# Moving the sigmoid of the state space gates from the gate products to the merge of the branches

## The chip, the cores and the metric

The kernel runs on one core of a Trainium2 chip. The metric is the device time of one execution in microseconds (us). Five engines work side by side, each taking its own instructions in order: TensorE (PE in the rows; PEld is its weight load), VectorE (DVE), ScalarE (ACT), GpSimd (POOL) and SyncE (SP). POOL, SP and ACT also issue DMAs; a "q" behind an engine's name (ACTq, POOLq) marks what its sequencer does without being busy.

## The reference, cut to what matters

A decoder layer for 256 tokens of width 2048 in float32. A state space branch and an attention branch read the same normed input; each is multiplied per channel by a sigmoid gate, and the sum goes through `w_out`.

```python
h = rmsnorm(x, attn_norm_w[l])
proj = h @ w_in[l]
z, xbc, dt_raw, q, k, v, g = jnp.split(proj, pts, axis=-1)
y_ssm = ssd_mixer(z, xbc, dt_raw, ...) @ w_ssm_out[l]
...
y_attn = moba_attention(q, k, v, ...) @ w_attn_out[l]
g_ssm, g_attn = jnp.split(jax.nn.sigmoid(g + b_gate[l]), 2, axis=-1)
x = x + (g_ssm * y_ssm + g_attn * y_attn) @ w_out[l]
...
x = x + (jax.nn.silu(u_gate) * u_up) @ w_down[l]
```

## The kernel before

**Weights.** All activations lie transposed, channels on partitions and 256 tokens along the row. Products are made in three passes so as to keep float32 precision: a weight is split in a rounded high part (`whi`, made by ACT at L180) and the remainder (`wlo`, made by DVE at L181), and TensorE does high by high (L212), high by low (L213) and low by high (L215). `unit` (L170) loads 1 MB of weights on SP's queue into one of three buffers `wraw` and splits it in two chunks of 1024 columns; `whi` and `wlo` have three buffers each, so ACT and DVE can work up to three chunks ahead of PE. One chunk is 24 matmuls.

**The stages.** First the attention branch, its gates (L561, `gate_attn`) and its output, which is stored pair by pair in DRAM (`ma`). Then the state space branch in nine steps (L837). Steps 0 to 7 make the projections of one of eight groups of heads (`group_units`) while the core work of the group before (`core_steps`: silu, transposes, decay by exponentials at L753, the output products at L769 and L770, a norm with a logarithm and an exponential at L299 and L300) is laid between the units by `sp.tick()`. The gates of this branch are 16 products: `gate_ssm` (L828), four in step 1, four in step 2 and eight in step 8, beside the core work of groups 0, 1 and 7. A gate ends with one activation on ACT (L831), from PSUM into half of a buffer `g`; each pair of gates (128 x 2 x 256) is stored to DRAM by POOL (L833, `gs`). ACT needs another table for a sigmoid than for an exponential or a silu; the line of an `ACT_TABLE_LOAD` is that of the activation it is for.

**The merge.** The last quarter of the product with `w_ssm_out` is eight units (L872), each with `merge` (L860) behind it. For pair u, POOL loads the stored gates `g` (L864) and the stored attention output `a` (L865); DVE adds the unit's sums to `yacc` (L866), multiplies by the gates (L867) and adds the attention part (L868); ACT rounds the result into `mt` (L869) and DVE makes its remainder (L870). `g` and `a` share three buffers, as `gpair` did before. So the gates of pair u+1 are loaded into the buffer that L870 of pair u-1 has just left, and `a` of pair u+1 into the one that L867 of pair u has left. Then follow the 16 units of `w_out` (L885), which read all 16 blocks of `mt`; of the first two units the first halves (blocks 0 to 7) are done before the second halves.

**The order.** The program gives the tiles and their dependencies; a planner sets the order on each engine ahead of time, by when it expects operands to be ready, earlier lines first among what is ready. An engine then takes its instructions in that order and waits where an operand is not there. The table loads are put in afterwards, before each activation whose table is not the loaded one.

Of the kernel before, what the change touches and what calls it, by code (L numbers as in the profile page):

```python
# [10 lines left out]
AF = mybir.ActivationFunctionType  # L11
# [147 lines left out]
def _body(tc, nc, d, out):  # L159
    V, S, PE = nc.vector, nc.scalar, nc.tensor  # L160
# [56 lines left out]
    def cm_unit(src, xh, xl, nk=16):  # L217
        parts = unit(src, nk * 128)
        ps = mm_tile()[:, :T]
        for c in range(2):  # L220
            cm_chunk(ps, parts[c], xh, xl, c * nk // 2, nk // 2, c == 0, c == 1)
        return ps
# [30 lines left out]
    def sm(name, i=0, n=1, rows=slice(0, 128)):  # L253
        o, _ = _SMALL[name]
        return small[rows, o + i:o + i + n]
# [297 lines left out]
    def gate_half(o):  # L553
        if o % 2 == 0:
            gpair[o // 2] = gate_pool.tile([128, 2, T], F32, name="g", bufs=3)
        return gpair[o // 2][:, o % 2]
# [38 lines left out]
    for o in range(KT):  # L595
# [4 lines left out]
        g = gl.pop(o)  # L600
# [16 lines left out]
    o = (KT + 10) * T  # L617
# [210 lines left out]
    def gate_ssm(o):  # L828
        pg = cm_unit(d["wgs"][o], hnh, hnl)
        g = gate_half(o)  # L830
        S.activation(g, pg, AF.Sigmoid, bias=sm("b_gate", o))  # L831
        if o % 2:
            nc.gpsimd.dma_start(gs[o // 2], gpair.pop(o // 2))  # L833

# [2 lines left out]
    for step in range(9):  # L837
        if step < 8:
            for i in group_units(step):
                sp.tick()  # L840
        outs = [(((step - 3) // 2), ((step - 3) % 2) * 4 + u) for u in range(4)] if step >= 3 else []
        ng = {1: 4, 2: 4, 8: 8}.get(step, 0)
        for _ in range(ng):
            gate_ssm(go)
            go += 1
            sp.tick()
        for q, u in outs:
            out_unit(q, u, acc_done(q))
            sp.tick()
        sp.flush()  # L850
        if step < 8:
            nu = 14
            if step == 7:
                nu = 10
            sp.add(core_steps(step), nu)
# [4 lines left out]
    def merge(u, ps):  # L860
        os_ = slice(2 * u, 2 * u + 2)
        g = gate_pool.tile([128, 2, T], F32, name="g", bufs=3)
        a = gate_pool.tile([128, 2, T], F32, name="g", bufs=3)
        nc.gpsimd.dma_start(g, gs[u])  # L864
        nc.gpsimd.dma_start(a, ma[u])  # L865
        V.tensor_tensor(yacc[:, os_], ps, yacc[:, os_], op=ADD)  # L866
        V.tensor_tensor(yacc[:, os_], yacc[:, os_], g, op=MUL)  # L867
        V.tensor_tensor(a, yacc[:, os_], a, op=ADD)  # L868
        S.activation(mh_[:, os_], a, AF.Copy)  # L869
        V.tensor_tensor(ml_[:, os_], a, mh_[:, os_].bitcast(F32), op=SUB)  # L870

    for u in range(8):  # L872
        out_unit(3, u, merge)
# [116 lines left out]
```

## Time and profile before

| | before |
|---|---|
| median of 3 runs | 2036.89 us (2035.17 to 2037.4) |
| the profiled execution | 2035.77 us, span of its instructions 2033.9 us |
| PE busy | 2026.2 us of the span |
| DVE, ACT, POOL busy | 1475.6, 1196.9, 43.4 us |
| DMA | 407.56 MB, 200 GB/s over the span |

A row of the timeline has the start, the duration, the engine, the line, the operation with its tiles and shapes, and in brackets how long the engine had been idle before it and what ended that. Matmuls are pipelined, so the distance between starts tells more of PE's pace than the duration of one. A stretch of PE is best measured from the start of one L215 group to that of the next, which is one chunk.

### The profile page before, as it was taken

The numbers are of one execution on the slowest core, as the hardware profiler recorded it, in microseconds if no ns is written. First come the engines' busy times: TensorE is split into PE (matmuls) and PEld (weight loads), VectorE is DVE, ScalarE is ACT, GpSimd is POOL, SyncE is SP. The second block draws the span as 40 slices with busy tenths as digits, with TensorE's granted clock in tenths as the row PEclk, the third lists the DMA queues.
The fourth block names the chain that finished last, engine by engine and source line by source line (L and its number), as shares of the span: only waits on it lengthen the run. The fifth ranks groups of instructions, "written<-read, shape, count | busy, mean of one in ns | idle before, by whom it ended". The sixth has DMA issues, their size and how long they took to land.

```text
span 2033.9 us, 39479 instructions
## 1 busy us (share of the span) xinstructions
PE 2026.2 (100%) x16539; PEld 1969.0 (97%) x16539; DVE 1475.6 (73%) x2225; ACT 1196.9 (59%) x1686; POOL 43.4 (2%) x83
## 2 busy tenths in 40 slices
PE   9999999999999999999999999999999999999999
PEld 7888889999999999999999999999999999999999
DVE  7567777556688898888989887677777765677554
ACT  6456556444668768667666755565555553455333
POOL 0000000000000000000000010000000000000000
PEclk9999999999999999999999999999999999999999
DMA  7654445655555556555565575555555555555554
GB/s 283 253 192 157 174 173 197 224 209 197 201 202 199 200 205 207 189 192 195 192 206 192 207 286 214 189 190 201 191 191 201 189 193 202 187 194 200 187 185 169
DMA packets 65690, 407.56 MB, mean 200 GB/s; under 512 B 7799, under 2 KB 10408, under 8 KB 21992
## 3 DMA queue, kind: packets, MB, share of 16 engines
q1 hardware_dynamic: 55384, 376.56, 51.5%
q0 software_dynamic: 6528, 22.12, 3.4%
q10 hardware_dynamic: 3600, 6.37, 0.9%
q8 instruction: 129, 2.11, 0.4%
q14 instruction: 49, 0.40, 0.1%
HBM read 398.63 MB, written 9.53 MB: 201 GB/s over the span
## 4 chain that ended last, share of the span: by engine, by line
PE 97%; ACT 1%; DVE 1%; DMA 0%; issue 0%; SPq 0%; DVEq 0%
PE mm L215 27%; PE mm L212 27%; PE mm L213 27%; PE mm L371 4%; PE mm L365 4%; PE mm L366 4%; PE cc L769 1%; PE cc L226 0%; PE cc L227 0%; PE cc L225 0%; DVE wlo L181 0%; PE cc L464 0%; PE cc L770 0%; PE cc L722 0%; ACT whi L180 0%; DMA wraw<-wv 0%
## 5 line engine op out<-in xcount | busy, mean ns | idle before, releaser
L180 ACT ACTIVATE whi<-wraw 128x1024 fp32r<-128x1024 f32 (+1 forms) x712 | 745.6, 1050 | 705.9 <-PE mm L213 556.8
L181 DVE TENSOR_TENSOR wlo<-wraw,whi 128x1024 fp32r<-128x1024 f32 (+1 forms) x712 | 858.7, 1209 | 275.7 <-ACT whi L180 270.7
L212 PE MATMUL mm<-hn,whi 128*128 128x256 f32 x1536 | 359.3, 277 | 1.7 <-ACT whi L180 1.7
L213 PE MATMUL mm<-hn,whi 128*128 128x256 f32 x1536 | 358.7, 276 | 0.0
L213 PE MATMUL mm<-fh,whi 128*128 128x256 f32 x1408 | 327.8, 276 | 0.0
L212 PE MATMUL mm<-fh,whi 128*128 128x256 f32 x1408 | 327.8, 276 | 0.0
L212 PEld LDWEIGHTS mm<-hn,whi 128*128 128x128 f32 x1536 | 288.4, 188 | 3.7 <-ACT whi L180 2.5
L213 PEld LDWEIGHTS mm<-hn,whi 128*128 128x128 f32 x1536 | 288.4, 188 | 0.1
L213 PEld LDWEIGHTS mm<-fh,whi 128*128 128x128 f32 x1408 | 264.3, 188 | 0.0
L212 PEld LDWEIGHTS mm<-fh,whi 128*128 128x128 f32 x1408 | 264.3, 188 | 0.0
L215 PE MATMUL mm<-hn,wlo 128*128 128x256 f32 x1536 | 205.9, 276 | 0.4 <-DVE wlo L181 0.4
L215 PEld LDWEIGHTS mm<-hn,wlo 128*128 128x128 f32 x1536 | 188.6, 188 | 0.8 <-DVE wlo L181 0.8
L215 PE MATMUL mm<-fh,wlo 128*128 128x256 f32 x1408 | 188.2, 276 | 0.0
L215 PEld LDWEIGHTS mm<-fh,wlo 128*128 128x128 f32 x1408 | 172.7, 188 | 0.0
L213 PE MATMUL mm<-a,whi 128*128 128x256 f32 x704 | 164.3, 276 | 0.0
L212 PE MATMUL mm<-a,whi 128*128 128x256 f32 x704 | 164.3, 276 | 0.0
L365 PE MATMUL mm<-whi,hp 128*128 128x512 f32 x384 | 152.1, 396 | 0.8 <-ACT whi L195 0.8
L366 PE MATMUL mm<-whi,hp 128*128 128x512 f32 x384 | 150.5, 392 | 0.0
L212 PEld LDWEIGHTS mm<-a,whi 128*128 128x128 f32 x704 | 132.1, 188 | 0.0
L213 PEld LDWEIGHTS mm<-a,whi 128*128 128x128 f32 x704 | 132.1, 188 | 0.0
L212 PE MATMUL mm<-yt,whi 128*128 128x256 f32 x512 | 119.4, 276 | 0.0
L213 PE MATMUL mm<-yt,whi 128*128 128x256 f32 x512 | 119.3, 276 | 0.0
(299 smaller groups left out, 3186.9 us busy)
## 6 DMA issues: line engine op xcount, KB each, us to landing
wraw<-wup SPq DMA_DIRECT2D x88, 1024.0 KB, 4.8
wraw<-wssd SPq DMA_DIRECT2D x80, 1024.0 KB, 4.8
wraw<-wqk SPq DMA_DIRECT2D x32, 1024.0 KB, 4.8
wraw<-wso SPq DMA_DIRECT2D x32, 1024.0 KB, 4.8
wraw<-wd SPq DMA_DIRECT2D x32, 1024.0 KB, 4.8
wraw<-wga SPq DMA_DIRECT2D x16, 1024.0 KB, 4.8
wraw<-wao SPq DMA_DIRECT2D x16, 1024.0 KB, 5.0
wraw<-wgs SPq DMA_DIRECT2D x16, 1024.0 KB, 4.8
```

The lines of the kernel that those rows point to most:

```text
L180: last_hi[0] = S.activation(hi[:, :n // 2], raw[:, s], AF.Copy)
L181: V.tensor_tensor(lo[:, :n // 2], raw[:, s], hi[:, :n // 2].bitcast(F32), op=SUB)
L212: PE.matmul(ps, w, xh[:, k0 + k], start=first and k == 0, stop=False)
L213: PE.matmul(ps, w, xl[:, k0 + k], start=False, stop=False)
L215: PE.matmul(ps, lo[:, k * 128:(k + 1) * 128], xh[:, k0 + k], start=False, stop=last and k == nk - 1)
L365: PE.matmul(pst[tt], hph[:, k0 + k, ts], wh, start=first and k == 0, stop=False)
L366: PE.matmul(pst[tt], hpl[:, k0 + k, ts], wh, start=False, stop=False)
L371: PE.matmul(pst[tt], hph[:, k0 + k, ts], wl, start=False, stop=last and k == 1)
L769: PE.matmul(ps, x0, m[:, :, h, 0:256], start=True, stop=False)
```

## The change

The gate's activation becomes an Identity with the same bias, so that what is stored in DRAM is the biased product. In `merge`, ACT applies the sigmoid in place to each pair of gates when it has been loaded, ahead of the three DVE operations of that pair.

```diff
@@ def gate_ssm(o):
         pg = cm_unit(d["wgs"][o], hnh, hnl)
         g = gate_half(o)
-        S.activation(g, pg, AF.Sigmoid, bias=sm("b_gate", o))
+        S.activation(g, pg, AF.Identity, bias=sm("b_gate", o))
         if o % 2:
             nc.gpsimd.dma_start(gs[o // 2], gpair.pop(o // 2))
@@ def merge(u, ps):
         nc.gpsimd.dma_start(g, gs[u])
         nc.gpsimd.dma_start(a, ma[u])
+        S.activation(g, g, AF.Sigmoid)
         V.tensor_tensor(yacc[:, os_], ps, yacc[:, os_], op=ADD)
         V.tensor_tensor(yacc[:, os_], yacc[:, os_], g, op=MUL)
         V.tensor_tensor(a, yacc[:, os_], a, op=ADD)
```

## Rows read from the trace of the kernel before

**Rows 1.** The page, part 1: busy us of each engine, share, instructions

```profile
PE 2026.2 (100%) x16539; PEld 1969.0 (97%) x16539; DVE 1475.6 (73%) x2225; ACT 1196.9 (59%) x1686; POOL 43.4 (2%) x83
```

**Rows 2.** Waits of PE: who waited for whom: us in total, times, longest

```profile
PE mm L212 <- ACT whi L180: 1.7, 2, 1.1
```

**Rows 3.** Timeline of PE, chunks in an undisturbed stretch of step 7

```profile
1052.12 1.07 PE L215 MATMUL mm<-hn,wlo 128*128 128x256 f32 x8
1054.84 1.07 PE L215 MATMUL mm<-hn,wlo 128*128 128x256 f32 x8
...
1058.29 1.07 PE L215 MATMUL mm<-hn,wlo 128*128 128x256 f32 x8
```

**Rows 4.** Timeline of PE in step 8: first and last chunk, the waits

```profile
1124.90 1.07 PE L215 MATMUL mm<-hn,wlo 128*128 128x256 f32 x8
...
1127.23 0.39 PE L212 MATMUL mm<-hn,whi 128*128 128x256 f32 x1 [0.56 <-ACT whi L180]
...
1132.13 0.38 PE L212 MATMUL mm<-hn,whi 128*128 128x256 f32 x1 [1.10 <-ACT whi L180]
...
1137.62 1.21 PE L215 MATMUL mm<-hn,wlo 128*128 128x256 f32 x8 [0.43 <-DVE wlo L181]
...
1155.81 1.07 PE L215 MATMUL mm<-hn,wlo 128*128 128x256 f32 x8
```

**Rows 5.** Timeline of PE in step 2, beside the gates there

```profile
690.66 1.07 PE L215 MATMUL mm<-hn,wlo 128*128 128x256 f32 x8
...
693.75 1.10 PE L215 MATMUL mm<-hn,wlo 128*128 128x256 f32 x8
```

**Rows 6.** Timeline of ACT in step 8, first and last of five table loads

```profile
1114.44 1.28 ACT L831 ACT_TABLE_LOAD   x1
...
1129.36 1.28 ACT L831 ACT_TABLE_LOAD   x1
...
1131.03 1.05 ACT L180 ACTIVATE whi<-wraw 128x1024 fp32r<-128x1024 f32 x1
```

**Rows 7.** Timeline of DVE in step 8

```profile
1127.21 1.23 DVE L181 TENSOR_TENSOR wlo<-wraw,whi 128x1024 fp32r<-128x1024 f32 x1 [1.37 <-ACT whi L180]
```

**Rows 8.** Groups of ACT by line: count, busy us, mean ns, idle before

```profile
L753 ACT ACTIVATE m<-m 128x768 f32<-128x768 f32 x32 | 26.9, 841 | 0.4
...
L682 ACT ACTIVATE slotA<-mm,small 128x256 f32<-128x256 f32 x24 | 13.2, 549 | 0.0
...
L831 ACT ACT_TABLE_LOAD x10 | 12.8, 1283 | 0.2
...
L753 ACT ACT_TABLE_LOAD x5 | 6.4, 1283 | 0.1
```

**Rows 9.** Timeline of one unit of the merge, DVE, POOL and ACT

```profile
1202.16 0.68 DVE L870 TENSOR_TENSOR mt<-g,mt 128x512 fp32r<-128x512 f32 x1
...
1203.13 0.54 POOL L864 DMA_DIRECT2D g<-gs  x1 [1.93 <-DVE mt L870]
...
1205.26 1.06 ACT L180 ACTIVATE whi<-wraw 128x1024 fp32r<-128x1024 f32 x1 [1.67 <-PE mm L213]
...
1206.58 0.63 ACT L869 ACTIVATE mt<-g 128x512 fp32r<-128x512 f32 x1 [0.25 <-DVE g L868]
...
1207.97 1.06 ACT L180 ACTIVATE whi<-wraw 128x1024 fp32r<-128x1024 f32 x1 [0.76 <-PE mm L213]
...
1210.57 0.69 DVE L867 TENSOR_TENSOR slotA<-slotA,g 128x512 f32<-128x512 f32 x1
1210.70 1.06 ACT L180 ACTIVATE whi<-wraw 128x1024 fp32r<-128x1024 f32 x1 [1.67 <-PE mm L213]
```

**Rows 10.** Loads of the gates at L864: us from issue to landing

```profile
DMA to landing us min/median/max: 5.6/5.8/6.8
```

**Rows 11.** Last L870 of the merge; a chunk of `w_out` on PE

```profile
1229.36 0.68 DVE L870 TENSOR_TENSOR mt<-g,mt 128x512 fp32r<-128x512 f32 x1
1229.48 1.07 PE L215 MATMUL mm<-mt,wlo 128*128 128x256 f32 x8
```

## The prediction, before the result was known

> **What bounds the kernel now.** I read the page's busy rows first: PE is busy for 2026.2 of 2033.9 us [rows 1], so the time is what TensorE has to compute plus the few places where it is kept waiting. No edit here touches a matmul. The whole question is which waits of PE go and which come. Second, the waits of PE: the largest is for the rounded weight halves that ACT makes at L180, 1.7 us in two places [rows 2]. Third, PE's timeline around those places. The yardstick is the distance from the first low-half matmul (L215) of one chunk of weights to that of the next: 2.72 us for a plain chunk, 3.45 us where the four matmuls of one pair of state-space heads stand between, so 0.73 us for these [rows 3]. In the last stage of the state space branch, 1124.90 to 1155.81, PE does nine chunks and the matmuls of four pairs: 9 x 2.72 + 4 x 0.73 = 27.40 us of work in 30.91 us [rows 4]. So 3.51 us are lost there. The three waits shown make 0.56 + 1.10 + 0.43 = 2.09 us of it; the other 1.42 us are restarts and matmuls that stand farther apart than elsewhere, whose cause no row shows. A second, smaller place is at 690.66: a chunk of 3.09 us, 0.37 us too long [rows 5].
>
> Fourth, ACT in that stretch. The two late halves follow on table loads: a gate (L831) loads the sigmoid's table, the next exponential of the decay (L753) loads its own again, 1.28 us each, five loads in turn from 1114.44 to 1129.36, and the rounding at 1131.03 stands behind them [rows 6]. PE takes it up at 1132.13 [rows 4]. Besides 690.66 this is the only place where a table load of the gates reaches PE.
>
> **Part 1: the gates lose their sigmoid.** The instruction stays, on the same tile with the same bias, so its own time hardly changes. Its table load goes: ten of 1.28 us, and with them the five that L753 needs to get the exponential back, 19.2 us of ACT in all [rows 8]. An Identity with a bias stands in the same stages at L682 [rows 8], and no table load has that line, so the new form costs no load. Of the 19.2 us only what held PE counts: the 3.51 us and, at most, the 0.37 us. Before the wait at 1132.13 ACT has by then spent five loads since 1114.44, 6.4 us; the waits of PE up to there come to 1.66 us, so ACT would be early. The wait for a low half at 1137.62 is DVE catching up after those late halves, so it should go too. Bounds for the gain: below, the 2.09 us of plain waits; above, 3.51 + 0.37 = 3.88 us. I take **3.5 us**, nearer to the upper end, since matmuls keep their distance where ACT is early [rows 3]; both ends stay in the range. What is late next there is DVE, which has the decay and the output products to do; but there it waits for ACT, not the other way about: 1.37 us ahead of the low half at 1127.21 [rows 7].
>
> **Part 2: eight sigmoids in the merge.** Each works on 128x512 in SBUF. The trace has no such sigmoid: the copy of the same width at L869, 0.63 us [rows 9], and an exponential of 768 columns, 0.84 us [rows 8], bound it; I take 0.65 us, by the copy. Eight make 5.2 us, and one table load 1.28 us. ACT has room: in a unit of 5.44 us (two chunks) it does two roundings of 1.06 us and one copy of 0.63 us [rows 9], 2.75 us, and would then do 3.4. By its length alone this part costs nothing; if the cover were gone it would cost 6.5 us.
>
> **Part 3: the wait that the sigmoid brings.** ACT takes its instructions in order, and now one of them waits for a load from DRAM. The load of the gates of pair u+1 is issued on POOL only when the buffer is free, 0.29 us after L870 of pair u-1 ends, at 1203.13 for example [rows 9]; it lands 5.6 to 6.8 us later, 5.8 in the median [rows 10], here at 1208.93. Its user L867 starts at 1210.57 [rows 9]. So there are 1.64 us between landing and use, and the sigmoid takes 0.65 of them: enough, if ACT turns to it then. Behind the waiting sigmoid stand the roundings of the next chunks, for which PE waits, and the copy L869, for which DVE waits, which for its part frees the buffer of the next load. What it costs hangs on its place in ACT's order, which the trace of before can't show. The four places within one unit are these, from rows 9:
>
> - after the rounding at 1207.97, before that at 1210.70: the data has landed, ACT is idle, nothing is late: 0 us.
> - between the copy at 1206.58 and the rounding at 1207.97: the sigmoid and then that rounding wait till 1208.93, some 1.4 to 1.6 us. A rounding has 0.9 + 2 x 2.72 - 1.06 = 5.3 us to spare, as it is made three chunks ahead. But DVE has its low half in front of L867, so the chain of loads gets 1.4 us later every second unit, 4.1 us by the last. The last L870 ends at 1230.04, and the second half of the first w_out unit, which starts 0.91 us after 1229.48, reads it as the last two of its eight blocks, twelve matmuls in, at 1231.75 [rows 11]: 1.7 us to spare. Cost 4.1 - 1.7 = 2.4 us.
> - ahead of the copy at 1206.58: a loop closes: L870, load 0.29 + 5.8, sigmoid 0.65, copy 0.63, L870 with gaps 0.8: 8.2 us a unit in place of 5.44. Six loads depend on it: 6 x 2.8 = 16.8 us late, less 1.7: **15 us**.
> - ahead of the rounding at 1205.26 as well: another 1.06 us a unit, 6 x 3.86 - 1.7 = 21.5 us.
>
> The loads of the second operand (L865) wait for L867 as before and move with it; POOL gets no instruction more. The first two pairs are loaded long before the stage; their sigmoids may stand in front of the last group's norm, for one table load and two sigmoids at most, 2.6 us of a chain that I can't price, taken as 0 with 2.6 left in the range.
>
> I take 0 us for part 3: the sigmoid's place is set where its operand is expected, and every earlier place needs the load to be expected within some 3.7 us of L870 (1202.84 to 1206.58), where the chip takes 6.1. But this is the weakest step.
>
> The Trainium skill (DMA: Bandwidth & Descriptors, Anatomy of one DMA) gives 2.0 us plus bytes over 436e3 for a load issued by GpSimd, an estimate of 2.6 us for these 256 KB. By that the operand would be there before the copy, the loop of the third place would be shorter than a unit and cost 0. The trace differs, with 5.8 us [rows 10], and the measurement decides.
>
> **The sum.** The profiled execution took 2035.77 us, 1.9 us around its span; the median of the three is 2036.89. From the median: 2036.89 - 3.5 + 0 = **2033.4 us**. About 0.2% (4.1 us, so below 2032.8 or above 2041.0) is what a measurement of this kernel can tell from no change; the whole gain lies at that bound.
>
> **Rivals.**
> - The sigmoid one place earlier, after the copy: 2036.89 - 3.5 + 2.4 = 2035.8. For it: the copy is the last work of a pair and ACT is idle behind it till 1207.97 [rows 9]. Chance 0.22.
> - Slower: the sigmoid ahead of the copy L869, so that the loop through the load sets the pace from the third pair on: 2036.89 - 3.5 + 15 = 2048.4, up to 2051. For it: the load is slow, 5.8 us [rows 10], so an order made with any shorter time in mind puts the sigmoid too early, and ACT is idle ahead of 1205.26 and of 1206.58 [rows 9]. Against it: only a time under 3.7 us does it. It decides from a place ahead of 1206.58. Chance 0.22; with the rounding behind it too, 2054.9, chance 0.10.
> - The gates do lose their table, but DVE holds PE in the same stretch, or as much is lost in front of the norm: 2036.9. Against it: DVE's own wait for ACT [rows 7]. Chance 0.10.
>
> **How the numbers follow.** The forecast has the remaining 0.36, its own range 2032.3 to 2035. Faster by over 0.2% needs the full upper bound of part 1: something under half of that, 0.17. Slower by over 0.2% is the two places ahead of the copy: 0.32. The rest, 0.51, is within. The range from 2032.2 to 2051 leaves out the 0.10 of the worst place and some 0.07 at its foot and in between.
>
> **What would show it.** Part 1: no table load at L831 or, between the gates, at L753; no wait of PE on L180 between 1112 and 1156, nine chunks and four pairs there in 27.4 us. Part 2: one sigmoid load in the merge. Part 3: ACT idle ahead of the new line, released by the load of g; its start against the copy L869; the distance between two L870, 5.44 or 8.2 us; PE's first w_out chunks waiting for the merge's tile. The forecast is wrong if PE waits in the merge at all.

## The result, and the profile after

The changed kernel takes **2051.19 us** in the median of six executions (2044.77 to 2056.58); the kernel before, beside it, takes 2035.65 us (2034.9 to 2037.4). The ratio is 1.0072 with the interval 1.005 to 1.0094: slower by 0.7%, some 15 us. Here and below a ratio leaves out executions in which the whole program ran markedly longer and a median does not, so the two can differ a little. The time lies 0.2 us above the upper end of the forecast's range, and of the four places listed in part 3 the trace shows the third and, for two pairs, the fourth.

The profiled execution took 2044.98 us with a span of 2043.2 us, one of the two shortest of the six. What is said below of its stretches explains 9.3 us over the span before (2033.9), not the median's 15. In the changed kernel the lines of the merge are one higher: the new sigmoid is L866, the operations on DVE L867 to L869, the copy into `mt` L870, its remainder L871.

The page, part 1 (busy us of each engine, share of the span, instructions):

```profile
PE 2029.5 (99%) x16539; PEld 1972.8 (97%) x16539; DVE 1475.9 (72%) x2225; ACT 1178.3 (58%) x1677; POOL 43.5 (2%) x83
```

Beside [rows 1], ACT has lost 18.6 us and nine instructions: eight sigmoids have come and, counted by line, 17 table loads have gone (the fifteen of [rows 8] and four at the norms, L299 and L300, less two new ones at L866). The span grew though ACT works less, so the waits come next. The waits (who waited for whom, us in total, times, longest):

```profile
PE mm L212 <- ACT whi L180: 8.0, 3, 4.0
...
ACT g L866 <- DMA g<-gs: 19.3, 6, 5.1
ACT L866 <- DMA g<-gs: 6.6, 1, 6.6
```

The second and third rows have no like before: the new line makes ACT stand still for 26 us, waiting for the load of the gates. The first is the row of [rows 2], 1.7 us then. ACT by line (count, busy us, mean ns, idle before and what ended it):

```profile
L866 ACT ACTIVATE g<-g 128x512 f32<-128x512 f32 x8 | 5.1, 632 | 19.3 <-DMA g<-gs 19.3
L866 ACT ACT_TABLE_LOAD x2 | 2.6, 1283 | 6.6 <-DMA g<-gs 6.6
```

No table load stands at L831 any more, where [rows 8] have ten, nor at L753. A sigmoid takes 632 ns.

**Where the time was won.** PE's timeline from step 8 to the first chunks of `w_out`; the first two rows are the ends of the stretch of [rows 4]:

```profile
1124.19 1.07 PE L215 MATMUL mm<-hn,wlo 128*128 128x256 f32 x8
...
1151.61 1.07 PE L215 MATMUL mm<-hn,wlo 128*128 128x256 f32 x8
...
1196.76 1.07 PE L215 MATMUL mm<-yt,wlo 128*128 128x256 f32 x8
1201.78 0.38 PE L212 MATMUL mm<-yt,whi 128*128 128x256 f32 x1 [3.95 <-ACT whi L180]
...
1204.78 1.61 PE L215 MATMUL mm<-yt,wlo 128*128 128x256 f32 x8
...
1208.12 1.10 PE L215 MATMUL mm<-yt,wlo 128*128 128x256 f32 x8
...
1230.73 1.10 PE L215 MATMUL mm<-mt,wlo 128*128 128x256 f32 x8
1235.22 0.39 PE L212 MATMUL mm<-mt,whi 128*128 128x256 f32 x1 [3.39 <-ACT whi L180]
...
1237.69 1.91 PE L215 MATMUL mm<-mt,wlo 128*128 128x256 f32 x8
...
1241.55 1.07 PE L215 MATMUL mm<-mt,wlo 128*128 128x256 f32 x8
```

The first two rows bound the same nine chunks and four pairs as in [rows 4]: 27.42 us, where 30.91 stood and 27.40 was reckoned. At 1151.61 PE is 1155.81 - 1151.61 = 4.20 us ahead of the kernel before: 3.49 us from this stretch and 0.71 that it already had at 1124.19.

**Where it was lost again.** The rest of that timeline, in stretches from one L215 to another, against 2.72 us a chunk (its first stretch is not among the rows shown):

| stretch of PE | takes | work | lost |
|---|---|---|---|
| 1170.89 to 1183.16, in front of the last group's norm | 12.27 | 4 x 2.72 | 1.39 |
| 1196.76 to 1204.78 | 8.02 | 2.72 | 5.30 |
| 1204.78 to 1208.12 | 3.34 | 2.72 | 0.62 |
| 1208.12 to 1230.73 | 22.61 | 8 x 2.72 | 0.85 |
| 1230.73 to 1237.69 | 6.96 | 2.72 | 4.24 |
| 1237.69 to 1241.55 | 3.86 | 2.72 | 1.14 |

The sum is 13.5 us; less the lead of 4.2 it is 9.3, the difference of the spans. Of the 13.5 us, 7.3 are the two long waits themselves (3.95 + 3.39); the other 6.2 are restarts, matmuls at a slower pace, and the first line.

**What held PE.** ACT's timeline in the merge:

```profile
1198.34 1.28 ACT L866 ACT_TABLE_LOAD   x1 [6.58 <-DMA g<-gs]
1199.63 0.63 ACT L866 ACTIVATE g<-g 128x512 f32<-128x512 f32 x1
1200.17 0.61 ACT L870 ACTIVATE mt<-g 128x512 fp32r<-128x512 f32 x1
1200.69 2.94 ACT L180 ACTIVATE whi<-wraw 128x1024 fp32r<-128x1024 f32 x3
...
1224.14 0.63 ACT L866 ACTIVATE g<-g 128x512 f32<-128x512 f32 x1 [4.02 <-DMA g<-gs]
1224.67 1.04 ACT L180 ACTIVATE whi<-wraw 128x1024 fp32r<-128x1024 f32 x1
1225.62 0.62 ACT L870 ACTIVATE mt<-g 128x512 fp32r<-128x512 f32 x1
...
1233.08 0.63 ACT L866 ACTIVATE g<-g 128x512 f32<-128x512 f32 x1 [4.94 <-DMA g<-gs]
```

Read the lines in order: a sigmoid of pair u+1 that waits for its load, and behind it the copy L870 of pair u. Of the six pairs that this concerns (2 to 7) five stand so; only pair 4's sigmoid comes behind the copy. For pairs 2, 5 and 7 the copy follows at once, as at 1200.17: the third place of part 3. For pairs 3 and 6 a rounding stands between, as at 1224.67: the fourth. At 1200.69 three roundings follow at one go: they had queued up behind the wait, and PE takes the first of them at 1201.78, 3.95 us late. The loop closes on DVE and POOL:

```profile
1219.20 0.69 DVE L871 TENSOR_TENSOR mt<-g,mt 128x512 fp32r<-128x512 f32 x1 [1.05 <-ACT mt L870]
1220.19 0.54 POOL L864 DMA_DIRECT2D g<-gs  x1 [2.83 <-DVE mt L871]
...
1226.89 0.69 DVE L871 TENSOR_TENSOR mt<-g,mt 128x512 fp32r<-128x512 f32 x1
```

L871 frees the buffer at 1219.89, POOL issues the load at 1220.19, the sigmoid starts at 1224.14, the copy at 1225.62, the next L871 at 1226.89: 7.69 us for one turn (with the rounding of 1224.67 in it), and 7.37 for the next, in place of 5.44 for a unit. All seven distances are 9.62, 6.95, 4.08, 7.36, 7.69, 7.37 and 4.80 us, 47.9 in all for 38.1. The last L871 starts at 1239.06, before it was 1229.36 [rows 11].

### The profile page after: what moved, and what is told of

Its sections match the earlier page's. It is cut to its first block, busy times and chain, and to the rows that moved or that the text cites. A ratio compares the mean times of both kernels' runs of the same rounds, so it can differ in the third digit from the quotient of the medians.

```text
span 2043.2 us, 39477 instructions
## 1 busy us (share of the span) xinstructions
PE 2029.5 (99%) x16539; PEld 1972.8 (97%) x16539; DVE 1475.9 (72%) x2225; ACT 1178.3 (58%) x1677; POOL 43.5 (2%) x83
## 4 chain that ended last, share of the span: by engine, by line
PE 95%; DMA 2%; issue 2%; DVE 1%; ACT 1%; POOL 0%; SPq 0%; DVEq 0%; ACTq 0%; POOLq 0%
PE mm L212 26%; PE mm L213 26%; PE mm L215 26%; PE mm L371 4%; PE mm L365 4%; PE mm L366 4%; DMA g<-gs 1%; PE cc L769 1%; PE cc L226 0%; PE cc L227 0%; PE cc L225 0%; DMA wraw<-wso 0%; PE cc L464 0%; PE cc L770 0%; PE cc L722 0%
## 5 line engine op out<-in xcount | busy, mean ns | idle before, releaser
L215 PE MATMUL mm<-hn,wlo 128*128 128x256 f32 x1536 | 205.5, 276 | 0.0
L215 PEld LDWEIGHTS mm<-hn,wlo 128*128 128x128 f32 x1536 | 188.4, 188 | 0.0
L215 PE MATMUL mm<-fh,wlo 128*128 128x256 f32 x1408 | 188.2, 276 | 0.0
L215 PEld LDWEIGHTS mm<-fh,wlo 128*128 128x128 f32 x1408 | 172.7, 188 | 0.0
```

The source lines that it names most:

```text
L215: PE.matmul(ps, lo[:, k * 128:(k + 1) * 128], xh[:, k0 + k], start=False, stop=last and k == nk - 1)
```

## The experiments

The theory to be tested: **the wait**. The gates' part of the change wins some 4 us, the sigmoid's length costs nothing, and the loss is ACT standing behind the load, by the place of the sigmoid in ACT's order. The rivals: **length and table**, that eight sigmoids and a table load more in the merge are what PE feels; and **lead paid back**, that what the gates give is lost again behind them, whatever the merge does. Every diff is against the changed kernel. Ratios are to the kernel before in the same rounds, whose median was 2036.24 us beside the experiments 1, 2, 3 and 4 and 2036.53 beside the others.

**1. The gates alone.** No sigmoid in the merge, so the sigmoid of these gates is left out of the computation altogether.

```diff
@@ def merge(u, ps):
-        S.activation(g, g, AF.Sigmoid)
```

> The gates' half of the change alone: the gates are stored without the sigmoid and the merge has no sigmoid either, so the sigmoid of the state space gates is left out of the computation. In the trace of the changed kernel PE reaches the first chunk of the last quarter at 1157.05, against 1161.24 before: 4.2 us early. Wait theory (the whole loss is ACT waiting in the merge for loads, because the sigmoid stands ahead of the copy of the pair before): 2035.7 - 4.2 = 2031.5 us, and no wait of PE from 1100 to 1240. Rival (the earlier lead comes only from work that has moved and is paid back later in the branch): 2035 to 2036 us. Either way no table load at L831 or L753.

Measured: 2032.42 us, ratio 0.9982 (0.997 to 0.9995), by the ratio 3.7 us faster. The waits of PE hold nothing of the stretch any more; these are all that are listed:

```profile
PE cc L267 <- DVE onesr L260: 1.1, 1, 1.1
PE mm L365 <- ACT whi L195: 0.7, 1, 0.7
PE cc L508 <- DVE sums L499: 0.2, 1, 0.2
```

The lead is kept to the end, so the third theory falls: 0.9982 lies off 1, and nothing is paid back behind the gates. The whole loss of the change, 1.0072 - 0.9982 = 0.0090 or 18.3 us by the ratios, hangs on the one line in the merge. The nine chunks and four pairs take 27.41 us here too (1126.00 to 1153.41), though PE enters them 1.10 us later than in the kernel before and leaves them 2.40 us earlier. So the 3.5 us of this stretch repeat, and the rest of the 4.20 us of lead in the changed kernel does not.

**2. The sigmoid behind a rounding.** All instructions, loads and buffers stay; the unit of pair u+2 is built within `merge` of pair u, and the sigmoid of pair u is put behind the first rounding of that unit. That is the first place of part 3, where the forecast had expected it. (The lines that keep hold of that rounding are left out of the diff.) One thing more moves with it, the unit's own place in the program; experiment 3 pins the sigmoid without that.

```diff
@@ def merge(u, ps):
-        S.activation(g, g, AF.Sigmoid)
+        ahead[u + 2] = unit(d["wso"][3, u + 2] if u < 6 else d["wout"][u - 6])
+        with tc.issue_after(first_hi[0].ins):
+            S.activation(g, g, AF.Sigmoid)
...
-        out_unit(3, u, merge)
+        out_unit(3, u, merge, ahead[u])
```

> The changed kernel with one order more: the sigmoid of pair u stands behind the first rounding of the unit two further on, so it is the place that the prediction priced at 0. Same instructions, same loads, same buffers. Wait theory: ACT reaches the sigmoid when the load has landed, its waits for g fall from 26 us to under 3, two L871 (the remainders of mt) stand 5.44 us apart again, 2031.5 us, up to 2033. Rival (the length of the eight sigmoids and their table load in a stage where DVE is 88% busy is what costs, or the load itself is too slow): as the changed kernel, 2045 to 2057 us.

Measured: 2032.2 us, ratio 0.9984 (0.997 to 0.9999). It is below both kernels, and with the sigmoid kept it is as fast as without one. What ACT waits for the gates, in all:

```profile
ACT g L871 <- DMA g<-gs: 2.0, 3, 0.8
```

And a unit on ACT's timeline (rounding L182, sigmoid L871, copy L875 in this kernel):

```profile
1197.00 0.63 ACT L875 ACTIVATE mt<-g 128x512 fp32r<-128x512 f32 x1 [0.25 <-DVE g L874]
1198.40 1.07 ACT L182 ACTIVATE whi<-wraw 128x1024 fp32r<-128x1024 f32 x1 [0.77 <-PE mm L216]
1200.29 0.63 ACT L871 ACTIVATE g<-g 128x512 f32<-128x512 f32 x1 [0.83 <-DMA g<-gs]
```

Copy, rounding, sigmoid: the load has had the copy and a rounding's time to land, and from the second on the remainders of the pairs stand 5.44 us apart again (5.63 for the last). The sigmoids of the first two pairs come behind the last group's norm here, at 1184.41 and 1188.49, so nothing is lost in front of it either. The same eight sigmoids and the same loads cost 19 us in one order and nothing in another. Length cannot be the cause.

**3. The sigmoid behind the copy.** The second place of part 3.

```diff
@@ def merge(u, ps):
-        S.activation(g, g, AF.Sigmoid)
+        with tc.issue_after(lastm[0].ins) if lastm[0] is not None else contextlib.nullcontext():
+            S.activation(g, g, AF.Sigmoid)
...
-        S.activation(mh_[:, os_], a, AF.Copy)
+        lastm[0] = S.activation(mh_[:, os_], a, AF.Copy)
```

> The changed kernel with the sigmoid of pair u put behind the copy into mt of pair u-1: one place later than in the changed kernel, and the second place of the prediction's list. Wait theory with that list: the gain of 4.2 us less 2.4 us, 2033.9 us (2032 to 2037), ACT waiting some 1.5 us for each load but not longer from pair to pair. Rival (length or load): 2045 to 2057 us. If the time is at 2045 or more, the loop through the copy is not what costs.

Measured: 2038.18 us, lowest 2035.41, ratio 1.0001 (0.9983 to 1.0018). That is 0.0019 over experiment 1, 3.9 us, with intervals that overlap. The median lies 1.2 us above the expected range; the ratio makes it 2036.4 us, within. Between the two profiled executions with a pinned order, this one and experiment 2, the difference is 2035.41 - 2031.88 = 3.5 us. Its waits and PE's timeline:

```profile
PE mm L212 <- ACT whi L180: 2.8, 1, 2.8
...
ACT g L869 <- DMA g<-gs: 8.4, 5, 2.4
```

```profile
1223.31 1.07 PE L215 MATMUL mm<-mt,wlo 128*128 128x256 f32 x8
1227.14 0.38 PE L212 MATMUL mm<-mt,whi 128*128 128x256 f32 x1 [2.77 <-ACT whi L180]
...
1229.08 1.07 PE L215 MATMUL mm<-mt,wlo 128*128 128x256 f32 x8
```

One chunk takes 5.77 us where 2.72 are due, at the end of the merge, as the list had it: ACT's 8.4 us of waits shift the chain a little with each unit till `w_out` is reached. The three orders give 0, 3.5 to 3.9 and some 18 us, for 2.0, 8.4 and 26 us of ACT's waits: the loss grows with the wait.

**4. Buffers of their own for the gates.** The load no longer waits for L871 of the pair before last; the order is left to the planner.

```diff
@@ def merge(u, ps):
-        g = gate_pool.tile([128, 2, T], F32, name="g", bufs=3)
+        g = sd.tile([128, 2, T], F32, name="ab", bufs=2)
```

> The changed kernel with the gates loaded into two buffers of their own (those of the decay rows, free by then), so that the load of pair u+2 is issued after L868 of pair u and no longer after L871; the attention part keeps the other three. The order is left to the planner. Wait theory: the load comes a whole unit earlier than it is used and the copy into mt no longer leads back to the load, so PE waits at most 1 us in the merge: 2031.5 to 2033 us. Rival (length): 2045 to 2057 us.

Measured: 2035.48 us, ratio 1.0008 (0.9981 to 1.0036): the loss of the change is gone, but the gain of the gates is not there, and the expectation missed by 2.5 us. ACT's waits for the gates are down to 2.9 us and none of PE's is listed in the merge. The order on ACT, however, came out otherwise, at the end of the merge and within it:

```profile
1214.92 1.07 ACT L180 ACTIVATE whi<-wraw 128x1024 fp32r<-128x1024 f32 x1 [0.76 <-PE mm L213]
1216.20 0.63 ACT L866 ACTIVATE ab<-ab 128x512 f32<-128x512 f32 x1 [0.21 <-DMA ab<-gs]
...
1229.83 0.51 ACT L897 ACTIVATE fh<-x,small 128x256 fp32r<-128x256 f32 x1 [4.80 <-DVE x L896]
```

```profile
1233.71 1.21 PE L215 MATMUL mm<-mt,wlo 128*128 128x256 f32 x8
1236.64 1.11 PE L215 MATMUL mm<-mt,wlo 128*128 128x256 f32 x8
...
1315.79 1.11 PE L215 MATMUL mm<-fh,wlo 128*128 128x256 f32 x8
1316.73 0.39 PE L284 MATMUL cc<-ssp,onesr 128*128 128x512 f32 x1
```

The planner itself has put the sigmoids of pairs 2 to 7 behind a rounding, the first place of part 3 (one is shown), and those of the first two pairs long before the norm, at 1129.91 and 1131.40. And the first operation of `w_out`'s epilogue (L897) now stands ahead of two roundings, so that ACT is idle for 4.80 us. PE comes through with one short interruption at 1233.71, and from there on runs 28 chunks in 79.15 us, 2.83 each, instead of 76.16: 3.0 us, though nothing waits. So the earlier start of the load took the loss away together with the order that made it; this kernel can't tell the two apart, and its new order has a price of its own.

**5. The sigmoid in both places.** The gates keep theirs (one sigmoid too many is computed), so nothing is won in step 8, and the merge is that of the change.

```diff
@@ def gate_ssm(o):
-        S.activation(g, pg, AF.Identity, bias=sm("b_gate", o))
+        S.activation(g, pg, AF.Sigmoid, bias=sm("b_gate", o))
```

> The merge's half of the change alone: the gates keep their sigmoid and the merge applies a second one to each loaded pair, so the values are not the reference's (a sigmoid too many). The table loads beside the gates stay. The order on ACT has the new sigmoid ahead of the copy into mt for most pairs, as in the changed kernel. Wait theory: the merge loses what it loses in the changed kernel, 13.7 us in its trace by my count (9.5 us net of a lead of 4.2), without the lead: 2045 to 2062 us, middle 2053. Rival (the changed gates are what upsets the merge): 2036 to 2038 us.

Measured: 2050.63 us, ratio 1.0072 (1.0048 to 1.0096). Part 2 and 3 alone, then, are worth +0.0072; with part 1's -0.0018 that makes +0.0054 where the whole change has +0.0072 (intervals of 0.002 on either side). By the ratios the two parts do not simply add, or the difference is chance. In the profiled executions they do: the span here is 14.0 us over that of the kernel before (2047.9 for 2033.9), with no lead to set off, where the change loses 13.5 behind its lead. The sign and the size of the loss are the merge's. The waits show its kind, beside 18.2 + 7.3 = 25.5 us of ACT for the load of the gates (the second figure ahead of a table load):

```profile
PE mm L212 <- ACT whi L180: 11.2, 6, 4.6
```

**6. The length and the table without the load.** In the merge ACT makes a sigmoid of the unit's sums in PSUM into a tile that nobody reads; the gates go without theirs, so the sigmoid of the gates is left out of the result and only the engine's time counts.

```diff
@@ def merge(u, ps):
-        S.activation(g, g, AF.Sigmoid)
+        S.activation(yz[:, 0:2], ps, AF.Sigmoid)
```

> The changed kernel with the eight sigmoids of the merge applied to the unit's product in PSUM and written to an unused tile, in place of the loaded gates: the same count, width and table load on ACT, but no load to wait for; the gates go into the merge without a sigmoid, so the output lacks it. Wait theory: the length is hidden, 2031.5 to 2033 us, as with the sigmoid left out. Rival (length and table load): 2045 us or more. It also bounds what the 6.4 us of ACT work cost by themselves.

Measured: 2033.42 us, 0.4 us over the expected range; ratio 0.9982 (0.9971 to 0.9994), the same as without any sigmoid. The one wait of PE in the merge:

```profile
PE mm L213 <- DVE mt L871: 0.2, 1, 0.2
```

Eight activations of that width and a table load are hidden: part 2's zero holds, and the rival of length and table falls.

**7. The load without the table.** An Identity in the merge's place of the sigmoid (the sigmoid is left out of the computation).

```diff
@@ def merge(u, ps):
-        S.activation(g, g, AF.Sigmoid)
+        S.activation(g, g, AF.Identity)
```

> The changed kernel with an Identity in place of the sigmoid in the merge, so the sigmoid of the state space gates is left out: the same instruction, waiting for the same load, in nearly the same order (ahead of the copy into mt for five of eight pairs), but no table load in the merge and none ahead of the last group's norm. Wait theory: the wait is the whole cost, 2043 to 2056 us. Rival (the switch of tables, three or four loads between the last gates and the end of the merge, is what costs): 2032 to 2035 us.

Measured: 2047.47 us, ratio 1.005 (1.0038 to 1.0062), with no table load at all in the merge.

```profile
ACT g L866 <- DMA g<-gs: 33.4, 7, 5.8
```

An operation of the same length that waits for the same load brings most of the loss back. By the ratios 0.0022, some 4.5 us, are missing to the change, at the edge of the two intervals. In the profiled executions it is the other way about: the span here is 2045.2 us for 2043.2 in the change, with 33.4 us of ACT's waits for 26 and all six pairs ahead of the copy. So no cost of the table loads is shown; what makes the difference of the ratios is open.

## Why the prediction was right or wrong

**What bounds the kernel: right.** Won and lost time are both places where PE stood or ran slow, and their sum is the difference of the spans.

**Part 1, the gates: right.** 3.5 us was reckoned from nine chunks and four pairs in 27.40 us; the changed kernel shows 27.42, experiment 1 27.41, and by its ratio experiment 1 gains 3.7 us. (The lead of 4.20 us lies over the upper bound of 3.88, by what differed ahead of the stretch.) The 1.42 us for which no row was there went with the waits, so taking the upper end was right. What they were, the trace of before shows with the result at hand:

```profile
1140.55 1.11 PE L215 MATMUL mm<-hn,wlo 128*128 128x256 f32 x8
1143.37 1.10 PE L215 MATMUL mm<-hn,wlo 128*128 128x256 f32 x8
```

Here, behind the three waits, a chunk takes 2.82 us instead of 2.72. That is PE's pace after an interruption, told in the last section; from 1137.62 to 1155.81 it makes some 0.65 us, and the restarts right behind the waits make the rest.

**Part 2, the length: right.** 0.65 us a sigmoid was reckoned, 0.632 is measured, and experiment 6 shows it hidden. Only the count of table loads was one short (four more at the norms, L299 and L300, went in exchange): there are two at the new line, since the last norm's own load at L299 comes between the sigmoids of the first two pairs and the others.

**Part 3, the place: wrong, and this is the step that failed.** The forecast took the first of four places, on the ground that the sigmoid's place is set where its operand is expected and every earlier place needs the load to be expected within some 3.7 us. The kernel has the third place for three of six pairs and the fourth for two. So the 3.7 us were not a reason against them; the prediction had said itself that an order made with a shorter time in mind does this, and gave it 0.22 and 0.10 of chance with the worse place. Why the planner chose it (too short a time for the load, or a rule of its own) no run shows. The runs show that these places were there, that pinning the first is worth 19 us, that an earlier load (experiment 4) made the planner itself take the first, and that the place lies open to the programmer.

By the Trainium skill (DMA: Bandwidth & Descriptors, Anatomy of one DMA) such a load would take an estimated 2.6 us, and the third place would have cost nothing. The loads of the gates in the changed kernel land after 3.0 us at the least, 5.1 in the median and 6.1 at the most, and the loop turns in 7.4 to 7.7 us against a unit of 5.44: the measurement decided, as the prediction had said.

**The price of the place: 15 us reckoned for the third and 21.5 for the fourth, 13.5 seen** in the profiled execution, 1.4 of them with the first two pairs, and 18.3 by the ratios between the change and experiment 1. The loop came out shorter, 7.4 to 7.7 us for 8.2, since the loads landed earlier: in the two turns told above the sigmoid started 3.95 and 5.20 us after the issue, where 5.8 was taken. Also, one pair of six escaped it. What the price lacked went the other way: the second and third roundings held up behind the first wait (5.30 us at 1196.76, where the list had only the end of the merge in view), PE's slow restart after each wait, and the norm.

**The first two pairs: 0 was taken, with 2.6 in the range; 1.4 us was lost.** ACT's timeline there:

```profile
1166.55 0.63 ACT L866 ACTIVATE g<-g 128x512 f32<-128x512 f32 x1 [5.06 <-DMA g<-gs]
1167.09 1.04 ACT L180 ACTIVATE whi<-wraw 128x1024 fp32r<-128x1024 f32 x1
1168.15 1.28 ACT L299 ACT_TABLE_LOAD   x1
```

Here "loaded long before the stage" was the mistake: the sigmoid of pair 1 waits 5 us for its load, with the last group's norm (L299) and a rounding behind it, and then the norm needs its table back.

**The list of places as a whole: right in its order and about its sizes,** as far as the runs show it; no run has the third or the fourth place by itself. Experiment 2 puts the first at 0, experiment 3 the second at 3.5 to 3.9 us (2.4 were reckoned, with overlapping intervals). What was wrong was the choice among them, made by an argument on the planner and from no row.

**A cure.** Experiment 2 is the change with its order written down: 2032.2 us, some 4 us under the kernel before and 19 under the change as it was made.

## What to carry to other kernels

An operation moved behind a load, onto an engine that works in order, puts everything behind it at that load's mercy: list what stands behind it for each place that it could take, price each place by the loop that it closes (buffer free, issue, landing, use, buffer free), and then write the order down rather than trust that the cheap place is taken. Look at the engine's order first when a change that removes work makes a kernel slower; here ACT did 18.6 us less and stood still for 26. And a gain that was proved in one stage (3.5 us) says nothing on the stage into which the work was moved.

## What the runs showed of the hardware

**A wait of TensorE costs more than its length.** Stretches of the changed kernel (PE busy and instructions, granted clock, DMA share, GB/s), after the wait of 3.95 us that ended at 1201.78:

```profile
1203.00:1206.00 3.00, 3.00 (x16) 0.51 0.81 240
1206.00:1209.00 3.00, 3.00 (x28) 1.00 0.98 376
```

For 3 us the granted clock is 0.51, the lower of its two levels (1.2 of 2.4 GHz), and 16 matmuls are done where 28 follow; some 1.5 us (3 x 0.49) are lost on top of the wait. Single matmuls show it:

```profile
1202.24 0.28 PE L213 MATMUL mm<-yt,whi 128*128 128x256 f32 x1
1202.36 0.28 PE L212 MATMUL mm<-yt,whi 128*128 128x256 f32 x1
...
1202.65 0.41 PE L212 MATMUL mm<-yt,whi 128*128 128x256 f32 x1
1202.86 0.41 PE L213 MATMUL mm<-yt,whi 128*128 128x256 f32 x1
```

The last two start 0.21 us apart; the first two, soon after the wait, still 0.12, so the clock fell only when PE was at work again. After the wait of 3.39 us at 1235.22 the same is seen, 0.50 from 1237 to 1240. The Trainium skill (TensorE: Matmul & The Clock Gate, Back-to-back issue gap) gives N/1.2 ns as the gap of a single matmul at the lower clock, an estimate of 213 ns for these 256 columns. The trace agrees with its 0.21 us.

**A slower pace without a lower clock.** After an interruption matmuls of the same shape may follow each other 0.118 us apart instead of 0.113, a chunk in 2.83 us instead of 2.72, while the granted clock is 1.00: eight chunks from 1208.12 in the changed kernel (22.61 us), and 28 in experiment 4, from 1236.64 to 1315.79, the last ahead of a matmul of 512 columns at L284. In experiment 3 it is a single chunk, from 1229.08. It is 0.11 us for a chunk and 3.0 us in experiment 4. What sets and ends it is not shown; no experiment was aimed at it.

**The scatter of the times is not explained.** The six executions of the changed kernel lie 11.8 us apart, those of the kernel before beside it 2.5; but the 35 executions of the kernel before beside the experiments 1 to 4 lie 10.2 apart (2034.83 to 2045.04). That the landing of the loads, 3.0 to 6.1 us, widens the scatter is not shown.
